# Background taps of the convolution: fewer with the token projections, more with the gate projections

## The chip, the cores and the metric

One NeuronCore of a Trainium2 chip runs the whole program in one launch. The time is what the device needs for one execution, in microseconds, as the median of several runs. Five engines work side by side, each through an instruction list of its own, in order: TensorE (PE, with the weight load PEld beside it), VectorE (DVE), ScalarE (ACT), GpSimd (POOL) and SyncE (SP), which issues the transfers between DRAM and on-chip memory. SBUF holds operands, and PSUM, eight banks here, takes what TensorE writes.

## The reference, cut to what matters

Two layers of a trunk over 512 latent tokens and 256 context tokens, model width 1024. Each layer normalizes its input, projects it to a convolution branch and two attention branches, weighs the branches by gates, and then runs a feed-forward part. What the change touches is the convolution branch and what is computed beside it:

```python
def conformer_conv(z_glu, p):
    a, g = jnp.split(z_glu, 2, axis=-1)                    # 2 x 512 channels
    y = a * jax.nn.sigmoid(g)
    y = depthwise_conv(y, p['conv_dw_w'], p['conv_dw_b'])  # 31 taps along the tokens
    y = jax.nn.silu(layer_norm(y, p['conv_ln_g'], p['conv_ln_b']))
    return y @ p['w_conv_out']

z = h @ p['w_in']
z_glu, z_qa, z_kva, z_kr, z_gq, z_gk, z_gv, z_gate = split_sections(z)
q_m = (rms_norm(z_qa, p['g_q_a']) @ p['w_q_b']).reshape(b, n, MLA_HEADS, MLA_QK)
...
gates = jax.nn.sigmoid(z_gate + p['b_gate']).reshape(b, n, N_BRANCH, D_MODEL)
merged = gates[:, :, 0] * br_conv + gates[:, :, 1] * br_mla + gates[:, :, 2] * br_gqa
```

In layer 0 the context tokens go through all of this too (768 tokens, as two segments of 512 and 256). In layer 1 they are needed only as keys and values, so the convolution, the queries and the gates have 512 tokens there.

## The kernel before, in words

**Matmuls and weights.** Every fp32 matrix product is three passes over high and low parts: x = hi + lo and w = hi + lo, and hi·hi, hi·lo and lo·hi are summed in PSUM. The `Feeder` streams the weights in the order of their use: a transfer into a `raw` tile, a copy of it to `hi` on ScalarE (L137), and `lo = raw - hi` on VectorE (L143). There are four buffers each for `raw`, `hi` and `lo`, and a block is split when an earlier block's buffer comes free, so the split of a block stands in VectorE's list wherever that release is written. TensorE must have the split to go on.

**Steps and the background.** The program is a list of steps, each with weight blocks, a function and a budget (two numbers, `add` in L175). The main loop takes a step's blocks, calls `pump` with the budget, then calls the function, and releases the blocks. `pump` (L205) is what places the convolution. It takes work from two queues: `bgq`, for VectorE, until its budget is at or below zero or a mark (`None`) comes, and `cvq`, for GpSimd, until the second budget is. The taps of channel groups 0 and 3 are in `bgq`: each is one instruction `acc += w*y` per segment (L146). Those of groups 1 and 2 are in `cvq`: ScalarE makes the scaled copy `ct` (L137), and GpSimd adds it to `acc` (L143). A tap's cost in the code is 1.06 and 1.9 (L516), times nT/768, so two thirds of it in layer 1. There are 30 such taps per group. Since engines run their lists in order, the budgets alone decide between which other instructions a tap stands.

**The order of the steps in a layer.**
- `glu`: eight blocks, the convolution's input (L531 to L596). The taps of a group are queued when its `y` is there.
- five latents `qa`, `kva` (L598); their squares are summed on ScalarE and VectorE (`SumSq`, L273).
- `tok` (L620), the token stage: the three blocks of `kkv`, then the four of `gq`. Six PSUM banks `tk` hold a sum each, one per 128 tokens, and after a projection's last block they are copied out (L140 is a copy by VectorE, L137 one by ScalarE). Ahead of the second `gq` block stand the column sums of the latents (`lat_rstd`, L644, with the matmuls in L256).
- `qproj` (L696), the query projection: three blocks, all needed from its first tokens on, budget zero. It queues the norms and rotations of the query heads (`q_post`, `g_post`, L715 and L751) in `bgq`.
- 24 gates (L870), each one block: 16 matmul groups of three passes, and a sigmoid by ScalarE (L879). In layer 0, 22 of them are followed by a piece of modulation (`mod`, L386), eight large matmuls.
- When a gate finds both queues empty, it queues the convolution's layer norm (`ln_start`, L801), whose sum `la` of the four groups feeds the matmul `mu` (L815).
- The attention and the feed-forward part follow, which the change doesn't touch.

**The budgets before.** `bud` is (4.5, 5.0) in layer 0 and (3.0, 2.5) in layer 1. The `glu` steps 2 and 3, `gq` and the gates have it; the latents have 1.5 less for VectorE; the three `kkv` blocks have (3.5, 3.0), (3.5, 3.0) and (0.5, 2.0).

Of the kernel before, what the change touches and what calls it, by code (L numbers as in the profile page):

```python
# [17 lines left out]
KD = D // 128  # L18
# [27 lines left out]


class Feeder:
    """Streams weight blocks: DRAM -> raw -> (hi, lo) split, ahead of their use."""

    def __init__(self, blocks, load, split):
        self.blocks, self.load, self.split = blocks, load, split
# [43 lines left out]
def trunk_kernel(ctx: ExitStack, tc: tile.TileContext, x_t, ctx_t, cc, vec, grow, ident, rope,  # L96
# [28 lines left out]
    def psum(s):  # L125
        return psp.tile([128, 512], F32, tag="ps", name=nm(s))
# [48 lines left out]
    def add(blocks, fn, budget=(0, 0)):  # L175
        steps.append(Step(blocks, fn, budget))

    def W(ap, n):
        return (ap, n, True)
# [282 lines left out]
    def layer(l):  # L462
        last = l == L - 1
# [3 lines left out]
        nq = 4 if last else 6  # L467
        nT = NX if last else T
        vv = vct
        bud = (3.0, 2.5) if last else (4.5, 5.0)  # L470

        def vcol(o):
            return vv[:, o:o + 1]
# [146 lines left out]
        def tok(wsrc, nb, kper, ncols, nt, evac, pre=None, tb=None):  # L620
            acc = {}
            for bi in range(nb):
                def fn(b, bi=bi):
                    H = st["H"]
                    hi, lo = b[0]
                    if bi == 0:
                        acc["p"] = [psum("tk") for _ in range(nt)]
                    if bi == 1 and pre:
                        pre()
                    kk = [k for k in range(bi * kper, min(KD, (bi + 1) * kper))]  # L630
                    for t in range(nt):
                        p, tc_ = acc["p"][t], slice(t * 128, (t + 1) * 128)
                        for i, k in enumerate(kk):
                            w = slice(i * ncols, (i + 1) * ncols)
                            hh, hl = H[k][0][:, tc_], H[k][1][:, tc_]
                            for q, (a, ww) in enumerate(((hh, hi[:, w]), (hh, lo[:, w]), (hl, hi[:, w]))):
                                mm(p[:, 0:ncols], lhsT=a, rhs=ww, start=(k == 0 and q == 0),
                                   stop=(k == KD - 1 and q == 2))
                        if bi == nb - 1:
                            evac(t, p)  # L640
                n = min(kper, KD - bi * kper) * ncols
                add([W(wsrc(bi, n), n)], fn, tb[bi] if tb else bud)
# [12 lines left out]
        def gq_evac(t, p):  # L655
            (cpA if t % 2 else cpV)(st["gt"][t][:, 0:512], p[:])
        tok(lambda bi, n: w_kkv[l, :, bi * 864:bi * 864 + n], 3, 3, 288, 6, kkv_evac,
            tb=((3.5, 3.0), (3.5, 3.0), (0.5, 2.0)))
        tok(lambda bi, n: w_gq[l, bi], 4, 2, 512, nq, gq_evac, lat_rstd)

        def rope_kr():
            rp = st["rp"].rearrange("p (t c) -> p t c", c=192)
# [202 lines left out]
        def gate_spill():  # L865
            for d, o in st.get("gs", []):
                dma(d, o)
            st["gs"] = []

        def gate(i):  # L870
            br, m = i % 3, i // 3

            def fn(b):
                gate_spill()
                pz = [(psum("gt"), s) for s in qseg]
                gemm(pz, ktiles(b[0], 0, KD), st["H"])
                for p, s in pz:
                    o = half("go")
                    act(out=o[:, 0:s[1]], in_=p[:, 0:s[1]], func=AF.Sigmoid, bias=vcol(V_BG + br * KD + m))  # L879
                    st["gs"].append((gate_d[l][m][br][:, s[0]:s[0] + s[1]], o[:, 0:s[1]]))  # L880
                if not (bgq or cvq or st.get("ln")):
                    st["ln"] = True
                    ln_start(None)
            add([W(w_gate[l, br * KD + m], 1024)], fn, bud)
        for i in range(24):
            gate(i)
            if i < 22:
# [778 lines left out]
```

## Time and profile before

| | us |
|---|---|
| median of 3 runs | 2550.24 (2550.2 to 2553.02) |
| the profiled execution: its span | 2548.6 |
| TensorE busy in it | 2395.1 (94%) |
| VectorE busy | 1612.0 (63%) |
| ScalarE busy | 1052.0 (41%) |
| GpSimd busy | 675.9 (27%) |

The shares are averages over stages with different limits: TensorE sets the pace nearly everywhere, and in the stages that this change touches, VectorE and GpSimd are much busier than the table says. Reading goes from the table to the waits of TensorE in a stretch (who waits, on which line, for whom), then to the list of the engine that was waited for (the timeline), and to the busy time and the granted clock by stretch. A clock of 0.50 in the rows is the lower of TensorE's two levels, 1.2 GHz, and 1.00 the higher, 2.4 GHz.

In layer 0 the token stage begins at 150 us, the query projection at 237.6 and the gates at 265.6, and they end at 504. In layer 1 these times are 1619, 1673, 1697.7 and 1851.

### The profile page before, as it was taken

Reading aid. Unit: us, or ns where it says so; the run is one execution under the profiler, and the core shown is the slowest. Engines: PE = TensorE matmul, PEld = TensorE weight load, DVE = VectorE, ACT = ScalarE, POOL = GpSimd, SP = SyncE. Lnnn points to the kernel's source line nnn. Section 1 sums busy time; section 2 is a strip of 40 time slices with the busy share of each in tenths; the row PEclk is TensorE's granted clock in tenths of the full one; section 3 lists DMA queues with packets and bytes.
Section 4 is the critical chain, followed back from the end, with each engine's and each line's share of the span. In section 5 each row is a group of like instructions: output and inputs, shape, how many; then the busy total and the mean of one; then the engine's idle time right before and its main releaser. Section 6 shows DMA issues by size and latency. Waiting matters only on the chain.

```text
span 2548.6 us, 33199 instructions
## 1 busy us (share of the span) xinstructions
PE 2395.1 (94%) x12538; PEld 1954.5 (77%) x12538; DVE 1612.0 (63%) x2669; ACT 1052.0 (41%) x1832; POOL 675.9 (27%) x505
## 2 busy tenths in 40 slices
PE   7977999988999999999999999888989999999999
PEld 4876777766778878888888887776766778888887
DVE  6889773389864465434344458889579865655454
ACT  3453422477751234323232234444376732434332
POOL 1575400136543221000000003433036541201000
PEclk9988999999999999999999999999999999999999
DMA  6111366611144412323322222233421154232332
GB/s 253 56 54 54 118 217 199 230 44 51 42 141 134 162 50 83 103 89 107 99 100 91 92 94 89 66 91 94 148 89 45 29 178 162 75 108 86 101 103 75
DMA packets 109197, 267.71 MB, mean 105 GB/s; under 512 B 20022, under 2 KB 28860, under 8 KB 109036
## 3 DMA queue, kind: packets, MB, share of 16 engines
q1 hardware_dynamic: 109036, 265.58, 31.8%
q8 instruction: 99, 1.62, 0.3%
q14 instruction: 62, 0.51, 0.1%
HBM read 231.31 MB, written 31.60 MB: 103 GB/s over the span
## 4 chain that ended last, share of the span: by engine, by line
PE 59%; DVE 22%; issue 10%; ACT 5%; DMA 2%; POOL 1%; SPq 0%; ACTq 0%; POOLq 0%; DVEq 0%
PE up L223 22%; PE pz L223 16%; PE bx L223 7%; DVE acc L146 6%; DVE lo L143 3%; PE gt L223 2%; DVE mx L998 2%; PE st L1148 2%; PE gl L223 2%; ACT hi L137 1%; PE qp L706 1%; DVE qm L146 1%; DVE rst L143 1%; PE mx L996 1%; PE ox L1177 1%
## 5 line engine op out<-in xcount | busy, mean ns | idle before, releaser
L143 DVE TENSOR_TENSOR lo<-raw,hi 128x1024 fp32r<-128x1024 f32 (+4 forms) x282 | 353.7, 1261 | 475.3 <-ACT hi L137 470.0
L137 ACT ACTIVATE hi<-raw 128x1024 fp32r<-128x1024 f32 (+4 forms) x298 | 283.2, 962 | 422.2 <-PE pz L223 170.9
L223 PE MATMUL up<-hl,hi 128*128 128x512 f32 (+1 forms) x1088 | 333.7, 354 | 6.1 <-DVE hl L146 5.8
L223 PE MATMUL up<-hh,hi 128*128 128x512 f32 (+1 forms) x1088 | 332.6, 353 | 2.0 <-DVE fc L146 2.0
L223 PE MATMUL up<-hh,lo 128*128 128x512 f32 (+1 forms) x1088 | 330.7, 352 | 0.8 <-DVE lo L143 0.8
L143 POOL TENSOR_TENSOR acc<-acc,ct 128x497 f32<-128x497 f32 (+14 forms) x180 | 236.3, 1335 | 283.9 <-ACT ct L137 280.7
L143 POOL TENSOR_TENSOR pl<-pe,ph 128x512 fp32r<-128x512 f32 x176 | 233.8, 1343 | 225.4 <-ACT ph L1157 81.1
L146 DVE SCALAR_TENSOR_TENSOR fc<-up,vct,fc 128x511 f32<-128x511 f32 (+1 forms) x264 | 162.1, 656 | 184.4 <-ACT fc L1485 182.6
L143 POOL TENSOR_TENSOR gl<-fc,gh 128x768 fp32r<-128x768 f32 (+1 forms) x44 | 69.3, 1574 | 784.0 <-ACT gh L137 681.5
L223 PEld LDWEIGHTS up<-hh,hi 128*128 128x128 f32 x1088 | 183.5, 190 | 42.7 <-ACT fc L1485 11.7
L223 PEld LDWEIGHTS up<-hl,hi 128*128 128x128 f32 x1088 | 184.4, 190 | 35.1 <-DVE hl L146 6.6
L223 PEld LDWEIGHTS up<-hh,lo 128*128 128x128 f32 x1088 | 185.3, 191 | 30.7 <-DVE lo L143 1.3
L223 PE MATMUL gt<-hh,lo 128*128 128x512 f32 x576 | 176.2, 360 | 15.5 <-DVE lo L143 15.5
L146 DVE SCALAR_TENSOR_TENSOR acc<-y,vct,acc 128x497 f32<-128x497 f32 (+14 forms) x180 | 185.1, 1074 | 1.6
L223 PE MATMUL gt<-hh,hi 128*128 128x512 f32 x576 | 178.4, 364 | 0.5 <-ACT hi L137 0.5
L223 PE MATMUL gt<-hl,hi 128*128 128x512 f32 x576 | 175.8, 359 | 0.0
L1485 ACT ACTIVATE fc<-up,vct 128x512 f32<-128x512 f32 (+1 forms) x132 | 88.4, 703 | 197.9 <-PE up L223 197.9
L223 PE MATMUL pz<-gl,hi 128*128 128x512 f32 (+1 forms) x528 | 163.5, 358 | 0.0
L223 PE MATMUL pz<-gh,hi 128*128 128x512 f32 (+1 forms) x528 | 163.0, 356 | 0.0
L223 PE MATMUL pz<-gh,lo 128*128 128x512 f32 (+1 forms) x528 | 162.7, 356 | 0.0
L1155 ACT ACTIVATE pe<-st 128x512 f32<-128x512 f32 x208 | 124.4, 599 | 76.5 <-PE st L1148 59.9
L998 DVE TENSOR_REDUCE mx<-mx 128x1 f32<-128x256 f32 (+1 forms) x288 | 139.3, 531 | 20.5 <-PE mx L996 20.2
(300 smaller groups left out, 4846.7 us busy)
## 6 DMA issues: line engine op xcount, KB each, us to landing
raw<-in_w_up_dram SPq DMA_DIRECT2D x88, 512.0 KB
raw<-in_w_mod_dram SPq DMA_DIRECT2D x80, 512.0 KB
raw<-in_w_gate_dram SPq DMA_DIRECT2D x48, 512.0 KB
raw<-in_w_a_dram SPq DMA_DIRECT2D x26, 512.0 KB
gd<-go SPq DMA_DIRECT2D x48, 256.0 KB
gx<-gd SPq DMA_DIRECT2D x48, 256.0 KB
raw<-in_w_dn_dram SPq DMA_DIRECT2D x32, 384.0 KB
raw<-in_w_dn_dram SPq DMA_DIRECT2D x32, 320.0 KB
```

Source lines behind the costliest of these rows:

```text
L137: act(out=o, in_=i, func=AF.Copy, scale=scale)
L143: e.tensor_tensor(out=o, in0=a, in1=b, op=op)
L146: V.scalar_tensor_tensor(out=o, in0=a, scalar=s, in1=b, op0=op0, op1=op1)
L223: mm(p[:, 0:cn], lhsT=w, rhs=a[:, c0:c0 + cn], start=(k == 0 and j == 0), stop=(k == n - 1 and j == 2))
L706: mm(p[i][:, 0:384], lhsT=a, rhs=w[:, i * 384:(i + 1) * 384], start=(k == 0 and q == 0), stop=(k == 2 and q == 2))
L996: mm(p[:, 0:n], lhsT=w, rhs=k[:, c0:c0 + n], start=True, stop=True)
L998: V.tensor_reduce(out=self.m2[:, o:o + 1], in_=p[:, 0:n], axis=AX.X, op=ALU.max)
L1148: mm(p[:], lhsT=a, rhs=b, start=(i == 0), stop=(i == len(ops) - 1))
L1155: act(out=e[:], in_=p[:], func=AF.Exp, scale=hd.scale)
L1177: mm(o[0:65, :], lhsT=vh, rhs=hi[:], start=(t == 0), stop=False)
L1485: act(out=acc[:, c], in_=p[:, 0:s[1]], func=AF.Identity, scale=vcol(o + 1), bias=vcol(V_FB + j + i * KF))
```

## The change

The change writes two more pairs of budgets beside `bud`: `tbud` for the token stage, which is (1.0, 1.9) in layer 0 and (1.0, 1.3) in layer 1, and `gbud` for the gates, (6.0, 6.0) and (4.0, 3.5). The first two `kkv` blocks get `tbud` and the third gets nothing; the first `gq` block gets nothing and the other three `tbud`; all gates get `gbud`. The budgets of `glu` and of the latents stay, and no instruction is added or removed. (A docstring of `Feeder` goes too, which moves nothing.)

```diff
@@ -467,7 +467,7 @@
         nq = 4 if last else 6
         nT = NX if last else T
         vv = vct
-        bud = (3.0, 2.5) if last else (4.5, 5.0)
+        bud, tbud, gbud = ((3.0, 2.5), (1.0, 1.3), (4.0, 3.5)) if last else ((4.5, 5.0), (1.0, 1.9), (6.0, 6.0))
 
         def vcol(o):
             return vv[:, o:o + 1]
@@ -655,8 +655,8 @@
         def gq_evac(t, p):
             (cpA if t % 2 else cpV)(st["gt"][t][:, 0:512], p[:])
         tok(lambda bi, n: w_kkv[l, :, bi * 864:bi * 864 + n], 3, 3, 288, 6, kkv_evac,
-            tb=((3.5, 3.0), (3.5, 3.0), (0.5, 2.0)))
-        tok(lambda bi, n: w_gq[l, bi], 4, 2, 512, nq, gq_evac, lat_rstd)
+            tb=(tbud, tbud, (0.0, 0.0)))
+        tok(lambda bi, n: w_gq[l, bi], 4, 2, 512, nq, gq_evac, lat_rstd, ((0.0, 0.0), tbud, tbud, tbud))
 
         def rope_kr():
             rp = st["rp"].rearrange("p (t c) -> p t c", c=192)
@@ -881,7 +881,7 @@
                 if not (bgq or cvq or st.get("ln")):
                     st["ln"] = True
                     ln_start(None)
-            add([W(w_gate[l, br * KD + m], 1024)], fn, bud)
+            add([W(w_gate[l, br * KD + m], 1024)], fn, gbud)
         for i in range(24):
             gate(i)
             if i < 22:
```

What it moves is shown by the order of VectorE's instructions in the built programs, at three places. The first is layer 0's token stage, from the split of one weight block (`lo`) on; `acc` <- `y` are taps of group 3, two instructions each (512 and 256 tokens less the tap's shift). Before:

```order
L143 TENSOR_TENSOR lo_1655<-raw_1308,hi_1654 128x1024
L146 SCALAR_TENSOR_TENSOR acc_1208<-y_1207,vct,acc_1208 128x502
L146 SCALAR_TENSOR_TENSOR acc_1208<-y_1207,vct,acc_1208 128x246
L146 SCALAR_TENSOR_TENSOR acc_1208<-y_1207,vct,acc_1208 128x503
L146 SCALAR_TENSOR_TENSOR acc_1208<-y_1207,vct,acc_1208 128x247
L146 SCALAR_TENSOR_TENSOR acc_1208<-y_1207,vct,acc_1208 128x504
L146 SCALAR_TENSOR_TENSOR acc_1208<-y_1207,vct,acc_1208 128x248
L146 SCALAR_TENSOR_TENSOR acc_1208<-y_1207,vct,acc_1208 128x505
L146 SCALAR_TENSOR_TENSOR acc_1208<-y_1207,vct,acc_1208 128x249
L143 TENSOR_TENSOR lo_1739<-raw_1396,hi_1738 128x1024
```

and now (`kr` and `gt` are copies out of the last `tk` bank):

```order
L143 TENSOR_TENSOR lo_1655<-raw_1308,hi_1654 128x1024
L146 SCALAR_TENSOR_TENSOR acc_1208<-y_1207,vct,acc_1208 128x502
L146 SCALAR_TENSOR_TENSOR acc_1208<-y_1207,vct,acc_1208 128x246
L143 TENSOR_TENSOR lo_1728<-raw_1396,hi_1727 128x1024
L146 SCALAR_TENSOR_TENSOR acc_1208<-y_1207,vct,acc_1208 128x503
L146 SCALAR_TENSOR_TENSOR acc_1208<-y_1207,vct,acc_1208 128x247
L143 TENSOR_TENSOR lo_1795<-raw_1484,hi_1794 128x1024
L140 COPY kr<-tk_1672 128x32
L140 COPY gt_1811<-tk_1672 128x256
L143 TENSOR_TENSOR lo_1855<-raw_1570,hi_1854 128x1024
L143 TENSOR_TENSOR lo_1903<-raw_1658,hi_1902 128x768
```

Between the first split and the next there were four taps, and there is one; the copies out of `tk` came after nine taps, and now come after two.

The second place is the first gates of layer 0, from the last copy of the query projection on; `qss` are the sums of squares of the query heads. Before:

```order
L140 COPY qm_2219<-qp_2330 128x384
L143 TENSOR_TENSOR lo_2353<-raw_2147,hi_2352 128x1024
L694 TENSOR_REDUCE qss_2358<-hs_2359 128x8
L694 TENSOR_REDUCE qss_2358<-hs_2362 128x8
L694 TENSOR_REDUCE qss_2358<-hs_2365 128x8
L694 TENSOR_REDUCE qss_2358<-hs_2368 128x8
L694 TENSOR_REDUCE qss_2358<-hs_2371 128x8
L694 TENSOR_REDUCE qss_2358<-hs_2374 128x8
L143 TENSOR_TENSOR lo_2454<-raw_2451,hi_2453 128x1024
L140 COPY rqb_2461<-rsy_2001 128x48
```

and now:

```order
L140 COPY qm_2114<-qp_2225 128x384
L143 TENSOR_TENSOR lo_2248<-raw_2052,hi_2247 128x1024
L146 SCALAR_TENSOR_TENSOR acc_1208<-y_1207,vct,acc_1208 128x507
L146 SCALAR_TENSOR_TENSOR acc_1208<-y_1207,vct,acc_1208 128x251
L146 SCALAR_TENSOR_TENSOR acc_1208<-y_1207,vct,acc_1208 128x508
L146 SCALAR_TENSOR_TENSOR acc_1208<-y_1207,vct,acc_1208 128x252
L146 SCALAR_TENSOR_TENSOR acc_1208<-y_1207,vct,acc_1208 128x509
L146 SCALAR_TENSOR_TENSOR acc_1208<-y_1207,vct,acc_1208 128x253
L146 SCALAR_TENSOR_TENSOR acc_1208<-y_1207,vct,acc_1208 128x510
L146 SCALAR_TENSOR_TENSOR acc_1208<-y_1207,vct,acc_1208 128x254
L146 SCALAR_TENSOR_TENSOR acc_1208<-y_1207,vct,acc_1208 128x511
L146 SCALAR_TENSOR_TENSOR acc_1208<-y_1207,vct,acc_1208 128x255
```

Six taps now stand between these two splits, and the head sums, which stood there, come after the last tap, some gates later.

The third place is in layer 1, at the convolution's layer norm. `gt` and `rt` are the last head's scaling and rotation, `la` and `lb` the sums of the four groups, and the last row is the first that reads `mu`. Before:

```order
L146 SCALAR_TENSOR_TENSOR gt_14714<-gt_14714,rsy_15552,gg 128x64 x8
L143 TENSOR_TENSOR rt_15780<-gt_14714,rp_14252 128x8x16 x4
L143 TENSOR_TENSOR gt_14714<-gt_14714,rp_14252 128x512
L143 TENSOR_TENSOR gt_14714<-gt_14714,rt_15780 128x512
L143 TENSOR_TENSOR lo_15822<-raw_15605,hi_15821 128x1024
L143 TENSOR_TENSOR lo_15862<-raw_15660,hi_15861 128x1024
L143 TENSOR_TENSOR la_15867<-acc_14049,acc_14241 128x512
L143 TENSOR_TENSOR lb_15868<-acc_14055,acc_14151 128x512
L143 TENSOR_TENSOR la_15867<-la_15867,lb_15868 128x512
L143 TENSOR_TENSOR lo_15901<-raw_15715,hi_15900 128x1024
L143 TENSOR_TENSOR lo_15935<-raw_15770,hi_15934 128x1024
L146 SCALAR_TENSOR_TENSOR acc_14049<-mu_15940,acc_14049 128x512
```

and now:

```order
L146 SCALAR_TENSOR_TENSOR gt_14695<-gt_14695,rsy_15598,gg 128x64 x8
L143 TENSOR_TENSOR rt_15752<-gt_14695,rp_14252 128x8x16 x4
L143 TENSOR_TENSOR gt_14695<-gt_14695,rp_14252 128x512
L143 TENSOR_TENSOR gt_14695<-gt_14695,rt_15752 128x512
L143 TENSOR_TENSOR lo_15794<-raw_15498,hi_15793 128x1024
L143 TENSOR_TENSOR la_15799<-acc_14049,acc_14241 128x512
L143 TENSOR_TENSOR lb_15800<-acc_14055,acc_14151 128x512
L143 TENSOR_TENSOR la_15799<-la_15799,lb_15800 128x512
L143 TENSOR_TENSOR lo_15833<-raw_15581,hi_15832 128x1024
L143 TENSOR_TENSOR lo_15867<-raw_15654,hi_15866 128x1024
L146 SCALAR_TENSOR_TENSOR acc_14049<-mu_15872,acc_14049 128x512
```

The work is the same, but one split fewer stands between the last head and `la`. On TensorE, `mu` stood ahead of gate 15 of this layer (counted from 0) and now stands ahead of gate 13; in layer 0 it moves from ahead of gate 14 to ahead of gate 16.

## Rows read from the trace of the kernel before

**Rows 1.** Waits of TensorE, 150 to 265.5 us: waiter <- releaser: us, times, longest.

```profile
PE cs L256 <- DVE gt L140: 11.6, 1, 11.6
PE tk L637 <- ACT ssq L281: 6.6, 1, 6.6
PE tk L637 <- ACT sq L286: 6.3, 1, 6.3
PE qp L706 <- DVE lo L143: 5.6, 2, 4.7
```

**Rows 2.** Timeline of VectorE, token stage, layer 0: start, us, operation, xcount, [idle before].

```profile
162.08 7.53 DVE L146 SCALAR_TENSOR_TENSOR acc<-y,vct,acc 128x497 f32<-128x497 f32 x6
...
208.29 0.41 DVE L140 COPY gt<-tk 128x256 f32<-128x256 f32 x1
...
239.93 5.25 DVE L146 SCALAR_TENSOR_TENSOR acc<-y,vct,acc 128x502 f32<-128x502 f32 x10
```

**Rows 3.** By stretch: start:end, us, busy (count) of the five, granted clock, DMA, GB/s.

```profile
201.30:214.90 13.60, 6.05 (x20) 5.37 (x21) 13.60 (x14) 6.16 (x11) 11.12 (x10) 0.50 0.19 69
242.30:252.40 10.10, 6.30 (x19) 5.81 (x20) 8.17 (x14) 0.49 (x1) 0.00 (x0) 0.50 0.32 101
1679.30:1689.40 10.10, 5.77 (x17) 5.27 (x18) 8.98 (x21) 0.49 (x1) 0.00 (x0) 0.50 0.39 108
```

**Rows 4.** Timeline of TensorE, the first gates of layer 0.

```profile
265.59 0.51 PE L223 MATMUL gt<-hh,hi 128*128 128x512 f32 x2
...
274.00 1.06 PE L386 MATMUL mod<-raw,cs 128*32 128x512 f32 x8
...
283.67 1.06 PE L386 MATMUL mod<-raw,cs 128*32 128x512 f32 x8
```

**Rows 5.** Timeline of VectorE, the first gates of layer 0.

```profile
267.26 1.23 DVE L143 TENSOR_TENSOR lo<-raw,hi 128x1024 fp32r<-128x1024 f32 x1 [1.09 <-ACT hi L137]
268.40 5.24 DVE L694 TENSOR_REDUCE qss<-hs 128x8 f32<-128x768 f32 x6
...
288.54 0.21 DVE L146 SCALAR_TENSOR_TENSOR rsy<-rst,rsy 128x48 f32<-128x48 f32 x1
...
298.20 1.92 DVE L146 SCALAR_TENSOR_TENSOR qm<-qm,rsy,gg 128x96 f32<-128x96 f32 x8
...
301.63 1.92 DVE L146 SCALAR_TENSOR_TENSOR qm<-qm,rsy,gg 128x96 f32<-128x96 f32 x8
```

**Rows 6.** Waits of TensorE, 265.5 to 504 us (gates of layer 0).

```profile
PE gt L223 <- DVE lo L143: 4.7, 3, 3.2
```

**Rows 7.** Timeline of GpSimd, the first gates of layer 0.

```profile
272.39 5.85 POOL L143 TENSOR_TENSOR acc<-acc,ct 128x511 f32<-128x511 f32 x6 [35.29 <-ACT ct L137]
```

**Rows 8.** Waits of TensorE in layer 1: 1618 to 1697.6 us, then 1697.7 to 1851.

```profile
PE qp L706 <- DVE lo L143: 9.0, 2, 7.5
...
PE gt L223 <- DVE lo L143: 10.8, 2, 7.7
```

**Rows 9.** Timelines of TensorE and ScalarE, the gates of layer 1.

```profile
1697.71 0.39 PE L223 MATMUL gt<-hh,hi 128*128 128x512 f32 x1
...
1772.93 0.69 ACT L879 ACTIVATE go<-gt,vct 128x512 f32<-128x512 f32 x1 [2.60 <-PE gt L223]
...
1778.37 0.69 ACT L879 ACTIVATE go<-gt,vct 128x512 f32<-128x512 f32 x1 [2.60 <-PE gt L223]
...
1797.82 1.26 PE L815 MATMUL mu<-la,ones 128*128 128x512 f32 x2 [2.87 <-DVE la L143]
```

**Rows 10.** Layer 1: the first gates by stretch, then rows of VectorE's timeline.

```profile
1702.80:1797.70 94.90, 81.34 (x339) 65.62 (x337) 91.77 (x223) 44.74 (x68) 37.17 (x26) 0.95 0.39 109
...
1640.57 8.51 DVE L146 SCALAR_TENSOR_TENSOR acc<-y,vct,acc 128x502 f32<-128x502 f32 x5
...
1681.94 3.06 DVE L146 SCALAR_TENSOR_TENSOR acc<-y,vct,acc 128x500 f32<-128x500 f32 x4
...
1797.08 0.69 DVE L143 TENSOR_TENSOR la<-la,lb 128x512 f32<-128x512 f32 x1
```

## The prediction, made before the changed kernel was run

> **What bounds the kernel now.** I read the table of busy shares first: TensorE is busy nearly throughout, so only the places where it stands still, or runs at its lower clock, are worth anything. The waits of TensorE in layer 0's token stage come next [rows 1]: four long waits in the stretch from 150 to 265 us. Two (6.3 and 6.6 us) belong to the latents, whose evacuations hold PSUM banks that the first token block needs. One of 11.6 us stands before the column sums, which need a bank that VectorE frees with a copy of a token tile, and 5.6 us stand in the query projection, for weight splits ("lo") that VectorE makes. Then VectorE's own list [rows 2]: that copy starts only at 208.29, since taps stand ahead of it, and one round of three taps (six instructions) takes 7.53 us while GpSimd adds its own taps, but five taps (ten instructions) take 5.25 us when GpSimd is still. So a tap costs 2.51 us beside a GpSimd tap and 1.05 us alone: **1.46 us is what a GpSimd tap costs VectorE in layer 0**. Last, the granted clock around the waits [rows 3]: it reads 0.50, the lower level, for 13.6 and 10.1 us, and TensorE is busy 6.05 and 6.30 us of them, at half its pace.
>
> **What the change does to the queues.** Counting with the costs in the code (1.06 and 1.9 a tap in layer 0, two thirds of that in layer 1; a budget is spent until it is at or below zero), the token block of layer 0 had 25 VectorE taps (4, 4, 1 and 5, 5, 5, 1 of a last call cut short by the end of the list) and 18 GpSimd taps, and now has 5 and 5. So 20 VectorE taps go into gates 0 to 3 (6, 6, 6, 2), and the gates have 28 GpSimd taps, four each in gates 0 to 6, where they had 15. In layer 1, 25 VectorE taps become 10, 15 go into gates 0 to 2, and the GpSimd taps in the gates go from 26 (two each in 13 gates) to 32 (three each in 11).
>
> **Layer 0, what is won.** The latents' budgets are untouched, so their two waits stay. Behind them VectorE reaches the copy after 2 taps and not 9, some 17 us sooner, before TensorE asks; and the splits for the query projection stand behind one tap each and not five. Both waits go: 11.6 + 5.6 = 17.2 us. With them go the stretches at the lower clock, half of 6.05 + 6.30, that is 6.2 us. Together 23.4 us, between 17.2 (the clock falls anyway) and 24.
>
> **Layer 0, what is lost.** A gate with its piece of modulation takes TensorE 9.67 us (from 274.00 to 283.67), gate 0 starts at 265.59 [rows 4]. Here a weight block is split only two gates ahead, so the split for gate i+2 stands in VectorE's list behind the background of gate i, and TensorE waits for it. I add up VectorE's list to the split of gate 7. It starts 2.8 us after gate 0 does (268.40) [rows 5]. Its own work: 20 taps at 1.05 = 21.0; 6 reductions at 0.87 (5.24 for six) = 5.2; the 17 small instructions of the norm's root at 0.24 (0.21 and the step to the next) = 4.1; four rounds of head scaling with rotation at 3.43 (298.20 to 301.63) = 13.7; six splits at 1.14 (267.26 to 268.40) = 6.8. That is 50.8 us. GpSimd has 24 taps issued by then and some of the next four; 26 at 1.46 = 38.0 (24 would be 35.0, 28 would be 40.9). So the split of gate 7 is there 2.8 + 50.8 + 38.0 = 91.6 us after gate 0 starts. TensorE would want it at 7 x 9.67 + 0.7 = 68.4, the 0.7 being the two matmul pairs ahead of the first that reads lo. It is 23.2 us late, and about 2 us go at the lower clock after the last wait (earlier ones are covered, since VectorE sets the pace): 25. From gate 8 on there is no GpSimd work and a gate's VectorE share, at most two such rounds and a split (8.0 us by the same durations), fits. The kernel before lost 4.7 us there [rows 6]. Loss 20.5, between 17 and 24. **Layer 0 comes out 3 us faster, between 7 faster and 7 slower.**
>
> The price of a GpSimd tap has a second reading. GpSimd alone takes 5.85 us for six instructions, 1.95 us a tap [rows 7], and VectorE loses 1.46 of it, so the two overlap in part. The Trainium skill, "SBUF — State Buffer", section "Who interferes with whom", says that a VectorE instruction with two SBUF inputs and a GpSimd one that reads SBUF hold the shared port one at a time, and the loser is blocked for the whole of the other. By that rule VectorE would lose 1.95 us a tap; the sum goes by the measured 1.46.
>
> **Layer 1, what is won.** The query projection's wait, 9.0 us [rows 8], has the same cause and goes, with half of the 5.77 us that TensorE was busy at the lower clock there [rows 3]: 11.9 us. The latents' wait stays here too.
>
> **Layer 1, what is lost.** There is no modulation in these gates; one takes 5.44 us (evacuations at 1772.93 and 1778.37), and they start at 1697.71 [rows 9]. VectorE is the bound here already: from 1702.8 to 1797.7 it is busy 91.77 of 94.9 us [rows 10], and TensorE waits 10.8 us for splits in it [rows 8]. At its end stands the sum "la" of the four convolution tiles, done at 1797.77, 100.1 us after the gates' start; TensorE waits for it with the matmul "mu" (2.87 us) [rows 9]. What decides is where "mu" stands: it was ahead of gate 15 and is now ahead of gate 13, since the larger budgets empty the background two gates sooner, and "la" has every tap and every head's scaling ahead of it in either case. So VectorE's whole list is due two gates earlier, though it is longer: 15 taps at 0.76 (3.06 for four without GpSimd) = +11.4, 6 more GpSimd taps at 0.94 (8.51/5 less 0.76) = +5.6, two splits fewer, -2.3 [rows 10]. "la" is done at 100.1 + 14.7 = 114.8. Behind "mu" come 11 gates where 9 came: + 2 x 5.44 = 10.9. Loss 14.7 + 10.9 = 25.6, between 20 (GpSimd's six taps free) and 28 (a longer stretch at the lower clock after the wait). **Layer 1 comes out about 13 us slower, between 8 and 17.** TensorE will stand before "mu" for about 15 us in place of 2.87.
>
> Nothing else is on the path: the number of instructions on each engine is unchanged, the weight loads keep their order on SyncE's queue and only the spills of the normed convolution move by a few gates, and their reload is in the attention's last heads.
>
> **Sum.** -3 + 13 = +10 us on the profiled execution's span of 2548.6 us. The runs' median of 2550.24 is 1.6 us above that span, so the time is 2560.
>
> **Rivals.**
> *GpSimd trails in layer 0* (0.13). ScalarE makes each scaled copy for GpSimd in its own order, behind the gate's evacuation and the squares, whose buffers VectorE's reductions give back. If that holds GpSimd up, so that at the split of gate 7 only 16 taps and not 26 have run, VectorE is 10 x 1.46 = 14.6 us earlier and the rest falls into gates where it has room: 2545, not slower. It decides at 19 taps, where the sum is level. Against it: 28 taps alone are 55 us, and eight gates last 77.
> *The gates take the taps for nothing* (0.05): only the gains remain, 23.4 + 11.9, and the losses that were there: 2515. Against it stands VectorE's full list in layer 1.
> *The token stage keeps its waits* (0.05), because ScalarE or GpSimd ends them and not VectorE: the losses alone, 20.5 + 25.6: 2596. Against it: the releasers [rows 1, 8] are VectorE's copy and splits.
> *Each GpSimd instruction costs VectorE all of itself* (0.05): 26 taps at 0.49 more in layer 0, 12.7 us: 2573. The Trainium skill's rule above would give that. The trace speaks against it, with 2.51 us for a pair of taps whose times alone add up to 3.0.
> That the change does not do what it says has no chance: the built order shows the taps in their new places.
>
> **How the numbers follow.** The forecast, 2560, has 0.72. Its own errors, some 5 us in each layer, put it within 0.2% (about 5 us, which is what a measurement of this kernel can tell from no change) in 0.16 and beyond it in 0.56. GpSimd trailing gives 0.07 same and 0.06 faster; the free gates 0.05 faster; the kept waits and the full block 0.10 slower. So faster 0.11, same 0.23, slower 0.66. The range 2546 to 2572 leaves out the free gates, the kept waits, a part of the trailing case and the forecast's tails.
>
> **What would show it.** In layer 0's token stage the waits before the column sums and the query projection are gone and the latents' two are there; gate 0 starts near 242. In its gates TensorE waits 20 to 25 us in all for "lo", most of it before gates 3 to 7, with the clock at 0.50 behind some. In layer 1 one wait of 12 to 18 us stands before "mu", ahead of gate 13. I am wrong if gate 8 of layer 0 starts no later after gate 0 than now, if "mu" waits under 5 us, or if the stretch from the first token matmul to the end of layer 1's gates is shorter than before.

## The result: slower by 0.89%, where 0.4% was forecast

The changed kernel takes 2573.87 us (median of four runs, 2569.54 to 2575.64) beside 2550.22 of the kernel before: a ratio of 1.0089, 95% interval 1.0075 to 1.0104. The forecast was 2560 in a range from 2546 to 2572: the direction was right, the size was not, and the time lies 1.9 us above the range.

The profiled execution has a span of 2573.9 us, 25.3 more than before. Taking the first matmul of each stage from the timeline of TensorE, the difference divides like this:

| stage | before, us | after, us | difference | forecast |
|---|---|---|---|---|
| start to the first token matmul, layer 0 | 150.9 | 151.6 | +0.7 | 0 |
| token stage and query projection, layer 0 | 114.7 | 91.8 | -22.9 | -23.4 |
| gates, layer 0 | 240.4 | 263.8 | +23.4 | +20.5 |
| attention and feed-forward, layer 0 | 1113.0 | 1123.0 | **+10.0** | 0 |
| token stage and query projection, layer 1 | 78.7 | 66.6 | -12.1 | -11.9 |
| gates, layer 1 | 154.6 | 178.3 | +23.7 | +25.6 |
| the rest | 696.3 | 698.8 | +2.5 | 0 |

The four terms of the sum came out within 3 us each. The fourth row, to which the prediction gave nothing, is the largest part of the miss.

The waits of TensorE in the changed kernel, in the stretches of [rows 1, 6, 8]: layer 0 up to its gates, its gates, then layer 1 up to its gates and its gates. The columns are as there.

```profile
PE tk L637 <- ACT ssq L281: 6.5, 1, 6.5
PE tk L637 <- ACT sq L286: 6.3, 1, 6.3
...
PE gt L223 <- DVE lo L143: 20.8, 4, 11.0
...
PE tk L637 <- ACT ssq L281: 5.9, 1, 5.9
PE tk L637 <- ACT sq L286: 1.4, 1, 1.4
...
PE gt L223 <- DVE lo L143: 21.2, 4, 8.4
PE mu L815 <- DVE la L143: 12.6, 1, 12.6
```

The waits before the column sums and in the query projections are gone (11.6, 5.6 and 9.0 us in [rows 1, 8]); the latents' waits have stayed. In the gates of layer 0, 4.7 us of waits for `lo` have become 20.8, and in layer 1 10.8 have become 21.2, with 12.6 before `mu` where there were 2.87.

VectorE's timeline in the changed kernel, from the split of gate 5 to that of gate 7 in layer 0, shows what its list is made of there:

```profile
297.11 2.12 DVE L143 TENSOR_TENSOR lo<-raw,hi 128x1024 fp32r<-128x1024 f32 x1 [4.38 <-ACT hi L137]
299.16 0.94 DVE L694 TENSOR_REDUCE qss<-hs 128x8 f32<-128x768 f32 x1
300.02 1.10 DVE L140 COPY rqb<-rsy 128x48 f32<-128x48 f32 x1
301.15 0.67 DVE L143 TENSOR_TENSOR qv<-qss,rqb 128x48 f32<-128x48 f32 x1
301.86 1.22 DVE L143 TENSOR_TENSOR qv<-qv,rqb 128x48 f32<-128x48 f32 x1
...
315.12 0.21 DVE L143 TENSOR_TENSOR rsy<-rsy,rqb 128x48 f32<-128x48 f32 x1
315.37 1.92 DVE L146 SCALAR_TENSOR_TENSOR qm<-qm,rsy,gg 128x96 f32<-128x96 f32 x8
...
334.62 2.25 DVE L143 TENSOR_TENSOR lo<-raw,hi 128x1024 fp32r<-128x1024 f32 x1
```

The 17 small instructions of the norm's root (the inverse square root of the head sums) take from 300.02 to 315.37. They need 0.2 us each, as the one at 315.12 does, but GpSimd is adding taps beside the others. Busy time by stretch (columns as in [rows 3]) has the lower clock behind the waits at 320 and 337, and GpSimd busy for 15 of the first 20 us:

```profile
300.00:320.00 20.00, 9.09 (x54) 6.80 (x52) 19.38 (x34) 9.00 (x17) 15.02 (x16) 0.79 0.29 98
320.00:340.00 20.00, 15.31 (x65) 12.06 (x66) 19.69 (x57) 8.21 (x18) 8.86 (x8) 0.76 0.60 197
```

The +10.0 us lie almost wholly in one place. From the first matmul of the attention's key and value projection (`pk`, right behind the gates) on, up to the same transpose in the attention, layer 0 took 115.0 us before and takes 123.7 after. Before, then after:

```profile
506.00:621.00 115.00, 98.28 (x464) 68.98 (x461) 100.06 (x205) 82.03 (x187) 59.36 (x52) 0.97 0.19 52
```

```profile
507.20:630.90 123.70, 103.71 (x465) 72.26 (x464) 102.49 (x208) 83.15 (x190) 59.47 (x53) 0.93 0.24 71
```

TensorE is busy 5.4 us longer, part of it at the lower clock (0.93 in place of 0.97), and idle 3.3 us longer. VectorE has three instructions more there.

### The profile page after: what moved, and what is told of

Its sections match the earlier page's. It is cut to its first block, busy times and chain, and to the rows that moved or that the text cites. A ratio compares the mean times of both kernels' runs of the same rounds, so it can differ in the third digit from the quotient of the medians.

```text
span 2573.9 us, 33203 instructions
## 1 busy us (share of the span) xinstructions
PE 2405.5 (93%) x12538; PEld 1959.8 (76%) x12538; DVE 1615.0 (63%) x2669; ACT 1050.8 (41%) x1832; POOL 676.5 (26%) x505
## 4 chain that ended last, share of the span: by engine, by line
PE 69%; DVE 19%; ACT 5%; issue 4%; DMA 1%; POOL 1%; SPq 0%; ACTq 0%; DVEq 0%; POOLq 0%
PE up L223 22%; PE pz L223 15%; PE gt L223 7%; PE bx L223 6%; DVE acc L146 5%; PE tk L637 4%; PE st L1148 2%; DVE lo L143 2%; DVE mx L998 2%; PE gl L223 2%; PE mod L386 1%; PE qp L706 1%; ACT hi L137 1%; PE mx L996 1%; PE ox L1177 1%
## 5 line engine op out<-in xcount | busy, mean ns | idle before, releaser
L146 DVE SCALAR_TENSOR_TENSOR acc<-y,vct,acc 128x497 f32<-128x497 f32 (+14 forms) x180 | 197.5, 1142 | 1.5
L223 PE MATMUL gt<-hl,hi 128*128 128x512 f32 x576 | 178.3, 364 | 0.0
L998 DVE TENSOR_REDUCE mx<-mx 128x1 f32<-128x256 f32 (+1 forms) x288 | 139.4, 531 | 23.4 <-PE mx L996 23.0
```

The source lines that it names most:

```text
L146: V.scalar_tensor_tensor(out=o, in0=a, scalar=s, in1=b, op0=op0, op1=op1)
L223: mm(p[:, 0:cn], lhsT=w, rhs=a[:, c0:c0 + cn], start=(k == 0 and j == 0), stop=(k == n - 1 and j == 2))
L998: V.tensor_reduce(out=self.m2[:, o:o + 1], in_=p[:, 0:n], axis=AX.X, op=ALU.max)
```

## The experiments

Each kernel ran beside the kernel before on its own chip, whose median was between 2551.4 and 2553.0.

**Where the ten microseconds behind layer 0's gates come from.** The order shows that the layer norm (`ln_start`) starts two gates later in layer 0, so that its end (the tail), the last spills (transfers of its result to DRAM) and the modulation's last transposes now stand in the attention's first heads: the last transpose was at 496.2 us, ahead of the first `pk` matmul at 506.0, and is now at 539.2, behind it. The first kernel makes just that of the kernel before:

```diff
+            if l == 0:
+                bgq.extend((None, None))
             bgq.append((2.6, a))
```

> The kernel before, with two marks put ahead of the convolution's layer norm in layer 0, so that its sums, its mu and everything behind it come two gates later (mu ahead of gate 16 in place of 14, and the last transposes of the modulation in the attention's first heads in place of gate 23), as in the changed kernel. No budget is changed. Theory A: the 8.8 us that the changed kernel loses in the first 115 us behind the gates of layer 0 come from this later tail alone. Then this kernel loses 7 to 10 us in the same stretch and comes to about 2559. Rival B: they come from where the stage begins in time and from the clock, and the tail is hidden. Then the stretch is the same within 2 us and the time is 2550 to 2552. Both expect the token stage, the query projection and layer 1 as before.

It took 2558.39 us, a ratio of 1.0021 (1.0012 to 1.0031), which is 5.4 us. Its stretch behind the gates:

```profile
506.80:629.40 122.60, 103.41 (x465) 72.27 (x464) 102.50 (x208) 83.29 (x190) 60.39 (x53) 0.93 0.25 72
```

122.6 us, with the busy times, the clock and even the instruction counts of the changed kernel. Theory A holds: no tap and no budget is needed to lose this. The gates themselves took 241.5 us, 1.1 more.

The reverse, on the changed kernel, takes one mark out behind the sums and one behind the root, in layer 0:

```diff
-            bgq.append((2.6, a))
-            bgq.extend((None, None))
+            bgq.append((2.6, a))
+            bgq.extend((None,) if l == 0 else (None, None))
...
-            bgq.append((2.6, d))
-            bgq.extend((None, None))
+            bgq.append((2.6, d))
+            bgq.extend((None,) if l == 0 else (None, None))
```

> The changed kernel, with two of the marks inside the layer norm of layer 0 taken out (one between the sums and mu, one between the norm's root and its use), so that its tail ends two gates sooner and the last transposes of the modulation are back ahead of gate 23. Theory A (the tail costs 8.8 us in the attention's first 115 us): that stretch is back within 2 us of the kernel before, less 1 to 3 us of new waits of TensorE in the gates where the marks stood: 2565 to 2567. Rival B (place in time and clock): the stretch still costs 7 us or more, 2572 to 2576.

> The same kernel as d2_ln_soon, for a second profile, since its profiled execution took 2559.6 us and its three others 2567 to 2572. If the attention's first 115 us of layer 0 are as long as in the kernel before (within 2 us) here too, theory A on the tail of the layer norm holds for both, and what differs between executions lies elsewhere; if they are 6 us or more longer in an execution of 2567 or more, the tail explains only a part.

The two profiled executions took 2559.62 and 2556.65 us, and in both the loss is gone:

```profile
505.90:619.70 113.80, 97.05 (x463) 67.83 (x461) 99.95 (x204) 81.99 (x187) 59.29 (x52) 0.99 0.18 53
```

```profile
501.00:616.10 115.10, 97.94 (x461) 68.68 (x459) 100.75 (x204) 81.39 (x187) 59.10 (x52) 0.97 0.18 52
```

The median is 2568.45, 1.0056 (1.0036 to 1.0077) of before: 15.5 us slower than the kernel before, where the changed kernel was 23.7, so 8.2 us came back. Three other executions took 2567 to 2572. None of those has a profile, so why they are some ten us longer than the two profiled ones is not known. That the tail costs, and that taking it out gives it back, is shown; that the 16 and 19 us between these two and the profiled execution of the changed kernel are all due to it is not.

Two further kernels divide the tail. One puts two marks ahead of the key heads' norms (`k_post`), which then stand in VectorE's list where the tail pushes them; the other moves the modulation's last transposes alone:

```diff
+            if l == 0:
+                bgq.extend([None] * 2)
             bgq.extend((0.6, a(t)) for t in range(6))
```

> The kernel before, with two marks ahead of the key heads' norms in layer 0's attention (k_post), so that they stand in VectorE's list where the changed kernel and d1_ln_late have them (some two units later). The layer norm's tail, its spills and the modulation's transposes stay in the gates. Theory A1: the tail costs in the attention because it is first in the queue there and pushes the key heads' norms back; then the attention's first 115 us of layer 0 take 6 to 9 us more, as in d1_ln_late (7.6), and the time is 2555 to 2559. Rival A2: what costs is the tail's own work there (four transposes on TensorE, the last spills and the loads behind them); then the stretch is the same within 1.5 us and the time is within 2 us of before.

```diff
-                bgq.append(None)
-                bgq.append((0.5, lambda: mod_tail(l, r, m)))
+                if (l, r) == (0, 2):
+                    st["mt"] = lambda: mod_tail(l, r, m)
+                else:
+                    bgq.append(None)
+                    bgq.append((0.5, lambda: mod_tail(l, r, m)))
...
+            if l == 0:
+                bgq.append((0.5, st.pop("mt")))
             bgq.extend((0.6, a(t)) for t in range(6))
```

> The kernel before, with one thing moved: the last transposes of the modulation in layer 0 (four on TensorE, two small instructions on VectorE) go from ahead of gate 23 to the head of the queue in the attention's first heads. The layer norm and its spills stay in the gates; the key heads' norms come one unit later. Theory A2 (the transposes cost there): the stretch takes 2 to 4 us more for them. Theory A1 (the key heads' norms are pushed back): one unit of the two, 2 to 5 us. If neither holds and the spills on SyncE's queue cost, the stretch is within 1 us of before.

The first took 2554.43 (1.0011, 1.0001 to 1.0020), with 120.0 us in the stretch; the second 2551.48 (0.9997, 0.9987 to 1.0007), with 118.5:

```profile
506.90:626.90 120.00, 100.74 (x462) 71.78 (x460) 100.13 (x205) 81.59 (x187) 58.13 (x52) 0.93 0.18 50
```

```profile
507.10:625.60 118.50, 99.72 (x469) 70.94 (x466) 102.05 (x207) 81.97 (x187) 56.59 (x52) 0.96 0.19 51
```

Pushing the key heads' norms back costs 5.0 us of the stretch in the profile and 2.6 by the medians, two thirds of the tail's price in the first kernel by the profile (7.6) and half by the medians (5.4), and without one instruction more in the stretch: that is A1 in part. For the transposes the profile says 3.5 us and the medians nothing. How the rest divides between transposes and spills stays open.

All profiles sort by the tail's place. From the first `pk` to the last `ox` <- `pl`, `vg` matmul of layer 0's attention, the five kernels whose tail reaches into the attention (the changed one, the first of this section and three of those below, with GpSimd cut short, with its taps in the token stage and with `mu` late in layer 1) took 146.6 to 149.1 us. The kernel before, the second of this section in both executions and the one below with the gates' budgets alone, whose transposes all stand in the gates, took 138.0 to 139.4, and the last two versions below, whose transposes stand there too, 140.2 and 141.4. The two that divide the tail lie between, at 144.3 and 142.7.

**What costs in the gates of layer 0.** The changed kernel, with GpSimd's additions in these gates cut to 16 columns, so that the rest of each tap is left out:

```diff
                             cpA(tmp[:, a0:a1], y[:, a0 + d:a1 + d], w)
+                            a1 = a0 + 16 if l == 0 and "Q" in st else a1
                             tt(P, acc[:, a0:a1], acc[:, a0:a1], tmp[:, a0:a1], ALU.add)
```

> The changed kernel, with GpSimd's additions of taps in the gates of layer 0 cut to 16 of the 512 or 256 columns: the same instructions, waits and ScalarE copies, but GpSimd is hardly busy there. (The rest of those taps is left out of the result.) Theory A: the waits for lo in these gates (20.8 us, and 3 us at the lower clock) come from what GpSimd's taps cost VectorE. Then they fall below 3 us, the gates of layer 0 take about 241 us in place of 263.8, and the root's small instructions (0.6 to 1.2 us each in the changed kernel) fall to 0.2. About 2551. Rival B: the twenty taps of VectorE that moved into gates 0 to 3 fill its list by themselves. Then waits of 10 us or more stay, 2561 or more.

It took 2546.37 us in its one execution, and the gates 236.6. The waits of TensorE in them, and the root in VectorE's timeline:

```profile
PE gt L223 <- DVE lo L143: 0.4, 1, 0.4
```

```profile
288.82 0.18 DVE L140 COPY rqb<-rsy 128x48 f32<-128x48 f32 x1
...
292.38 0.21 DVE L143 TENSOR_TENSOR rsy<-rsy,rqb 128x48 f32<-128x48 f32 x1
292.62 1.93 DVE L146 SCALAR_TENSOR_TENSOR qm<-qm,rsy,gg 128x96 f32<-128x96 f32 x8
```

The root takes 3.8 us in place of 15.4, and the waits are gone, with all twenty moved taps of VectorE still there. So the price is that of GpSimd's additions, as the sum had it: VectorE's own list alone was due in time.

Next, the taps of GpSimd stay in the token stage, and only VectorE's move:

```diff
-            tb=(tbud, tbud, (0.0, 0.0)))
+            tb=((tbud[0], 3.0), (tbud[0], 3.0), (0.0, 2.0)))
...
-lat_rstd, ((0.0, 0.0), tbud, tbud, tbud))
+lat_rstd, ((0.0, bud[1]),) + ((tbud[0], bud[1]),) * 3)
```

> The changed kernel, with GpSimd's budgets in the token stage put back to those of before: 18 GpSimd taps of layer 0 and 16 of layer 1 stay in the token stage, and only VectorE's taps (20 and 15) move into the gates. Theory A (a GpSimd tap costs VectorE some 1.5 us in layer 0 wherever VectorE is the one that TensorE waits for, and nothing in a token stage that has 20 VectorE taps fewer): the token stage and the query projection keep their gain, 20 to 23 us in layer 0 and 12 in layer 1; in the gates of layer 0 the split of gate 7 comes 2.8 + 50.8 + 15 x 1.46 = 75.5 us after gate 0 where 68.4 is wanted, so 7 to 9 us of waits in place of 20.8, and the stage takes about 250; in layer 1 the gates take 172 to 174 in place of 178.3. About 2555. Rival B: what counts is that GpSimd runs at all beside VectorE's small instructions, not how many taps it has: the gates of layer 0 stay above 258, 2565 or more. Rival C: the GpSimd taps that stay delay the copies and splits of the token stage, and 8 us or more of its waits come back.

2550.46 us, 0.9994 (0.9984 to 1.0003) of before. TensorE's waits up to the gates of layer 0, then in its gates, then in the gates of layer 1:

```profile
PE tk L637 <- ACT sq L286: 6.3, 1, 6.3
PE tk L637 <- ACT ssq L281: 6.2, 1, 6.2
PE qp L706 <- DVE lo L143: 2.2, 2, 1.6
...
PE gt L223 <- DVE lo L143: 5.6, 3, 4.3
...
PE gt L223 <- DVE lo L143: 15.9, 4, 8.3
PE mu L815 <- DVE la L143: 14.7, 1, 14.7
```

The token stage and the query projection of layer 0 took 97.1 us, 17.6 less than before, where 20 to 23 were expected: 2.2 us of waits for the query projection's splits are back, which is rival C on a small scale. The gates of layer 0 took 245.3 and those of layer 1 171.9, a little less than theory A said. Twenty VectorE taps more, with the larger budgets, cost the gates of layer 0 4.9 us; thirteen GpSimd taps on top of them cost 18.5.

**What the budgets cost without any moved tap.** The kernel before, with `gbud` in the gates:

```diff
-            add([W(w_gate[l, br * KD + m], 1024)], fn, bud)
+            add([W(w_gate[l, br * KD + m], 1024)], fn, gbud)
```

> The kernel before with the larger budgets of the gates alone; the token stage has its taps as before, so no tap of VectorE moves and the gates' other work comes sooner. mu of layer 0 stands ahead of gate 10 in place of 14, that of layer 1 ahead of gate 11 in place of 15. Theory A (what costs in layer 1 is that mu's sum is due sooner, with the same work ahead of it): the sum is done some 95 us after the gates' start, 13 gates of 5.44 come behind it in place of 9, so layer 1's gates take 165 to 173 us in place of 154.6; in layer 0 VectorE has room and the gates stay within 4 us of 240; the token stage is as before; 2561 to 2570. Rival B: larger budgets cost nothing without the moved taps, 2548 to 2553.

2580.75 us, 1.0110 (1.0095 to 1.0125): no better than the whole change, with no tap of the token stage moved. The attention of layer 0 took 1112.8 us, as before, since the tail stays in the gates: the loss is in the gates of both layers. TensorE's waits in the gates of layer 0 and of layer 1:

```profile
PE gt L223 <- DVE lo L143: 10.0, 6, 4.4
PE gt L223 <- ACT hi L137: 1.6, 1, 1.6
...
PE gt L223 <- DVE lo L143: 22.1, 5, 9.8
PE mu L815 <- DVE la L143: 5.2, 1, 5.2
```

Layer 1's gates took 172.8 us, within the expectation. Layer 0's took 252.3, where 240 plus or minus 4 was expected: a miss. VectorE's and GpSimd's timelines show why. GpSimd now has four taps a gate, eight additions, and two such gates fall on the root:

```profile
274.04 0.18 DVE L140 COPY rqb<-rsy 128x48 f32<-128x48 f32 x1
274.25 0.67 DVE L143 TENSOR_TENSOR qv<-qss,rqb 128x48 f32<-128x48 f32 x1
274.95 1.21 DVE L143 TENSOR_TENSOR qv<-qv,rqb 128x48 f32<-128x48 f32 x1
...
288.08 1.76 DVE L143 TENSOR_TENSOR lo<-raw,hi 128x1024 fp32r<-128x1024 f32 x1
...
304.46 2.25 DVE L143 TENSOR_TENSOR lo<-raw,hi 128x1024 fp32r<-128x1024 f32 x1
```

```profile
272.86 7.78 POOL L143 TENSOR_TENSOR acc<-acc,ct 128x511 f32<-128x511 f32 x8 [33.71 <-ACT ct L137]
281.10 7.65 POOL L143 TENSOR_TENSOR acc<-acc,ct 128x507 f32<-128x507 f32 x8 [0.46 <-ACT ct L137]
```

The root takes 14.0 us, and behind it three rounds of head scaling stand ahead of the next split. The work is no more than before; it is due sooner.

**What the place of `mu` costs in layer 1.** The changed kernel, with `mu` two gates later in layer 1 alone:

```diff
             bgq.append((2.6, a))
-            bgq.extend((None, None))
+            bgq.extend((None, None) if l == 0 else (None,) * 4)
```

> The changed kernel, with two more marks between the sums and mu in layer 1 alone: mu stands ahead of gate 15 again, as in the kernel before, and all taps stay where the change put them. Theory A (the prediction's): what the larger budgets cost in layer 1 is that mu's wait comes two gates sooner. Then the wait of 12.6 us before mu falls to 0 to 3, the gates of layer 1 take some 10 to 11 us less, 2563. Rival B: VectorE is behind in these gates in any case, and the splits for gates 13 and 14 come as late as mu's sum did: TensorE waits for lo in place of mu, and the time stays within 3 us of 2574.

2564.42 us, 1.0046 (1.0031 to 1.0061). Layer 1's gates took 168.6 us in place of 178.3, and the waits in them are:

```profile
PE gt L223 <- DVE lo L143: 25.6, 5, 8.4
```

The wait before `mu` is gone and the waits for `lo` have grown from 21.2 to 25.6: theory A by size (9.7 us where 10 to 11 was expected), with a part of rival B.

**A version that beats both.** If the price is what is due early, and not the sum of the work, the layer norm should not stand behind the heads, and GpSimd's taps should stay in the token stage. The version below gives the layer norm a queue that `pump` serves first:

```diff
+        while lnq and bv > 0:
+            x = lnq.popleft()
+            if x is None:
+                break
+            x[1]()
+            bv -= x[0]
         while bgq and bv > 0:
...
-                if not (bgq or cvq or st.get("ln")):
+                if not (st["taps"] or cvq or st.get("ln")):
```

(`st["taps"]` counts VectorE's taps not yet issued, and all of `ln_start` goes to `lnq`.)

> A version drawn from the runs so far. The token stage keeps few VectorE taps (budget 1.0) but GpSimd's as before. The layer norm of the convolution gets a queue of its own, which pump serves first, so it starts when the last tap is issued and no longer waits for the heads' norms and rotations; the heads' work spreads over all 24 gates, with gate budgets of (4.0, 5.0) in layer 0 and (3.0, 2.6) in layer 1. mu stands ahead of gate 7 in layer 0 and of gate 11 in layer 1, and the last transposes of the modulation ahead of gate 23. Theory A (waits in the gates come from what is due early in VectorE's list, not from its sum): the token stage and the query projection take 22 us less in layer 0 and 12 in layer 1, the gates of layer 0 take 235 to 243, those of layer 1 142 to 152, the attention begins without a tail: 2505 to 2520. Rival B: VectorE has no room in layer 1's gates at all (taps, heads, splits and what GpSimd costs it exceed 131 us), and mu's sum is due four gates sooner than before: the gates of layer 1 take 165 or more, 2525 or more.

2524.23 us, 0.9878 (0.9855 to 0.9900): 4 us above the expected range. It differs from the kernel that left GpSimd's taps in the token stage (2550.46) by the queue and the smaller gate budgets; which of the two gives how much of the 26.2 us was not run. Layer 0's gates took 237.6 us, layer 1's 159.1, where 142 to 152 was expected; there 10.1 us of waits for `lo` and 7.3 before `mu` remain. The second version also relieves the latents (one of its three changes):

```diff
-            add([W(w_a[l, blk], 1024)], fn, (bud[0] - 1.5, bud[1]))
+            add([W(w_a[l, blk], 1024)], fn, (bud[0] - 1.5 if key == "qa" else 0.0, bud[1]))
```

> v1_own_queue with three more changes. The last two latents get no VectorE tap (they had three each), since their evacuations stand in VectorE's list behind those taps and TensorE waits for the squares that follow them (6.3 and 6.8 us in layer 0, 1.4 and 5.9 in layer 1). The token stage takes 8 VectorE taps in place of 5, none ahead of the last splits; the gates take three more. In layer 1 the gates' budget is (2.8, 2.6) and mu stands ahead of gate 12 in place of 11. Theory A: the two waits at the token stage's start fall to under 3 us in each layer, which gives 10 to 15 us in layer 0, clock included, and 5 to 8 in layer 1; the gates of layer 0 stay at 236 to 242; those of layer 1 are between 150 and 160: 2495 to 2510 beside 2524. Rival B: the waits at the token stage's start are ScalarE's (its copies for GpSimd stand there too) and stay; then 2520 to 2528.

2505.69 us, **0.9815 (0.9799 to 0.9831)**. Its waits of TensorE in layer 0's token stage, then in layer 1's, then in layer 1's gates:

```profile
PE tk L648 <- ACT sq L292: 6.3, 1, 6.3
PE tk L648 <- ACT ssq L287: 1.4, 1, 1.4
PE cs L262 <- DVE gt L140: 1.1, 1, 1.1
...
PE tk L648 <- ACT ssq L287: 2.7, 1, 2.7
PE tk L648 <- ACT sq L292: 1.4, 1, 1.4
...
PE gt L229 <- DVE lo L143: 5.1, 2, 3.6
PE mu L826 <- DVE la L143: 3.2, 1, 3.2
```

One of the two long waits of each latent stage fell beside the first version, from 6.8 to 1.4 us and from 5.9 to 2.7; the other of layer 0, 6.3 us, stayed, against the expectation. The gates took 239.1 and 151.2 us. The 151.2 hold a new wait of 4.3 us behind the last gate, where TensorE's transposes for the attention ask for a head that VectorE has not done: the heads' work, spread over all gates, now ends late.

## Why the prediction was right in sign and wrong in size

**The gains.** Forecast 23.4 and 11.9 us, measured 22.9 and 12.1. That VectorE's list, and not ScalarE or GpSimd, ended these waits is shown by the kernel that left GpSimd's taps in place: 17.6 and 12.3 us of the gain were there.

**Layer 0's gates.** Forecast 20.5, measured 23.4, and by the mechanism of the sum: waits for `lo` of 20.8 us in four places from gate 3 to gate 7 and three stretches at the lower clock, behind those of gates 3, 6 and 7 (the granted clock was 0.57 from 277 to 280 us and 0.50 from 320 to 323 and from 337 to 340). The split of gate 7 was done 93.5 us after gate 0 began (334.62 + 2.25 less 243.4), where 91.6 was forecast. A part of that agreement is luck: VectorE stood idle for 4.4 us on the way, for a copy by ScalarE, which the sum did not have; with its own 50.8 us of work, that leaves some 35.5 us for GpSimd in place of 38.0. The price of 1.46 us for a GpSimd tap was read from pairs of taps; the root's small instructions, which the prediction priced at 4.1 us and charged with the same 1.46 a tap, gave 15.4 us beside some eight taps, 1.4 a tap. With GpSimd's additions cut short nothing of the loss is left.

**Layer 1's gates.** Forecast 25.6 in two parts, 14.7 for the longer list and 10.9 for `mu` two gates sooner; measured 23.7. `mu` began, with `la` just done, 112.8 us after the gates did, where 114.8 was forecast, 12.7 later than before, and 11.0 us more came behind it. With `mu` moved back 9.7 us come back and 14.0 remain, so both parts were sized rightly. Their place was not: the prediction had one new wait of about 15 us before `mu`, and there are 12.6 there and 10.4 us more for `lo` ahead of it, since VectorE falls behind before its list reaches the sum.

**The step that failed** is the sentence that nothing else is on the path, because "only the spills of the normed convolution move by a few gates". The change moves everything that stands behind the taps in the queue. `mu` of layer 0 was seen to go from gate 14 to gate 16, and no term was made of it. The tail behind it then reaches into the attention, where its own work and the key heads' norms that queue behind it meet a stretch in which TensorE was idle for 16.7 of 115 us already. This was +8.7 us in the profiled stretch; the same shift alone, in the kernel before, costs 7.6 us there and 5.4 by the medians. With the tail sooner, the changed kernel's median is 2568.45, inside the range of the forecast. By the profiles the miss is 14.5 us (25.3 where the four terms add up to 10.8): 10.0 in this stage, 2.9 in layer 0's gates and 2.5 at the end of layer 1, less 0.9 in the other rows. The 2.5, and 1.3 of the stage that lie outside the stretch, have no cause that the runs show; the changed kernel's own executions lie 6 us apart.

**What the prediction charged to the wrong thing** is a part of layer 0's loss. It worked it out from the taps that arrive in these gates. The larger budgets alone, with none arriving, lose 11.9 us there: the 15 GpSimd taps of before come in fewer gates and fall on the root. How much of the changed kernel's 23.4 this is stays open, since its list is another. Where the VectorE taps arrive and GpSimd's do not, the loss is 4.9 us. In layer 1 the budgets alone lose 18.2 us, with `mu` four gates sooner: there the prediction had charged the budgets too, in its second part.

**The rivals.** GpSimd did not trail, the gates did not take its taps for nothing, and the token stage did not keep its waits. That a GpSimd instruction costs VectorE all of itself would have given 2573, which is close to the result, but not for its reason. Layer 0's gates would have lost 33.2 us by it and lost 23.4, and with the larger gate budgets alone the root took 10.2 us more than without GpSimd and the split behind it 0.5 more, for eight taps, which is 1.34 a tap, and the tap itself takes 1.95 [rows 7].

## What to carry to other kernels

A budget for background work in a queue moves everything behind it too. Follow the queue to its last entry, and price the stage into which its end now falls, before saying that nothing else is on the path. Where one engine slows another that is waited for, put its work where the other has time, and let a chain with long latencies start as soon as its inputs are there, in a queue of its own: the same instructions, ordered so, take 1.85% less.

## What the runs showed of the hardware

VectorE's small instructions are held at GpSimd's pace. In the kernel with larger gate budgets alone, GpSimd's eight additions take 7.78 and 7.65 us, 0.96 to 0.97 us each, as they do alone [rows 7], while VectorE's 48-wide instructions beside them take 0.67 and 1.21 us in turn instead of 0.2: about one passes for each addition. Beside VectorE's taps both sides lose. In the kernel whose GpSimd taps stayed in the token stage, VectorE's timeline has twelve tap instructions at 12.47 us beside GpSimd, and the root without it at 3.8 us:

```profile
251.47 12.47 DVE L146 SCALAR_TENSOR_TENSOR acc<-y,vct,acc 128x507 f32<-128x507 f32 x12
...
303.97 0.17 DVE L140 COPY rqb<-rsy 128x48 f32<-128x48 f32 x1
...
307.76 1.92 DVE L146 SCALAR_TENSOR_TENSOR qm<-qm,rsy,gg 128x96 f32<-128x96 f32 x8
```

In the kernel with GpSimd's additions cut short the same twelve take 6.41 us:

```profile
244.80 6.41 DVE L146 SCALAR_TENSOR_TENSOR acc<-y,vct,acc 128x507 f32<-128x507 f32 x12
```

And GpSimd's eight additions beside the 12.47 us take 1.31 us each:

```profile
251.04 10.49 POOL L143 TENSOR_TENSOR acc<-acc,ct 128x511 f32<-128x511 f32 x8 [24.41 <-ACT ct L137]
```

The Trainium skill, "SBUF — State Buffer", section "Who interferes with whom", says that where the two contend for the port they share, the one that issues second waits for the whole of the other's instruction. For the small instructions the rows agree: each waits for about one addition. As a price of GpSimd's work it is too high here, 1.95 us a tap by the rule and 1.34 to 1.46 measured, since one of VectorE's own instructions is done for each addition.
